# A transformer layer on one core: the causal mask moves from a PE product to a GpSimd clearing, with deeper rings and fewer VectorE operations in the first stage

## Chip, core and metric

One core of a Trainium2 chip runs the whole layer. The metric is the device time of one execution in microseconds; the kernel before takes 2691.55 us (median of three runs, 2686.87 to 2695.32). The engines are TensorE (PE, matmul), VectorE (DVE), ScalarE (ACT), GpSimd (POOL) and SyncE (SP, which here only issues DMAs). Each takes its instructions in order.

## What is computed

One layer over 2048 positions of width 1024, in float32, cut to what matters here:

```python
a = rms_norm(h, pre_mix_g)
q, k, v, f, u_sg, v_sg = split(a @ w_in)
c = cumsum(log_sigmoid(f + f_bias))                     # per head
logits = q @ k.T * 64 ** -0.5 + c[t] - c[s]             # 8 heads of 64, causal
y_att = softmax(where(k_pos <= q_pos, logits, -inf)) @ v
u, v = gelu(u_sg), layer_norm(gelu(v_sg), ln_g, ln_b)
y_sg = u * (tril(w_s) @ v + b_s)                        # chunks of 128 positions
h = h + rms_norm(concat(rms_norm(y_att), rms_norm(y_sg)) @ w_out)
h = h + rms_norm(square(relu(rms_norm(h) @ w1)) @ w2)
h = h + sigmoid(h @ w_g + b_g) * (p @ w_pe)
```

## The kernel before

Products are done in three parts (`mm3`, L104 to L106): each operand is split into a rounded high half and the rest, and high x high, high x low and low x high are summed. ACT makes the high half of a weight (L96), POOL the low half (L100); of a value that comes out of PSUM, ACT makes the high half (L116) and DVE the low half (L117).

**First stage** (up to about 565 us): the projection by `w_in`, in four blocks of 512 positions. Each block has six groups of columns (`GROUPS`, L326) of four accumulations; the first three (344 wide) give the gating value `gv`, a mixed one, and the forget logits with the rest of `u`; then come q, k and v (512 wide). In the text a "group" counts these accumulations, 0 to 23, two PSUM places (`pacc`) turn about. What else a block does hangs on that count: the layer norm from accumulation 8 (L409 to L418), the square sums and scaling of the next block's rows from 11 (`x_norm`, L279 to L296), the log-sigmoid at 11 (L374 to L393), the gating products from 14. The forget logits get their bias on DVE as they come out of PSUM (L357), and the gelu of the same accumulator follows on ACT (L358). The raw weights go through three places (`wrp`), results on their way to DRAM through two (`stg`).

Between these matmuls `maxima` (L142) is interleaved for the block before: it finds each query's largest logit. It loads key tiles (`KM`, two places, L165) and query tiles (`QM`) by DMAs on ACT's queue, multiplies (L169), and DVE takes maxima from PSUM (L172; on the diagonal tile the part left of the diagonal square by L172, and the square itself, plus the mask `dmask`, by L175).

**Second stage** (about 565 to 1115 us): attention, the output projection, and the maxima of the last block. `scores` (L637) does one tile of 128 keys by up to 512 queries: two products into PSUM (L644, L647), on a diagonal tile (`by_pe`, all four blocks since `MASKB` is 4) a third one that adds `dmask` (L649), the exponential on ACT (L651), its high half on ACT or DVE (L659, L657), the low half on DVE (L660). `weigh` (L663) multiplies by the values (L672 to L674). Scores run four steps ahead (`LA`); PSUM has two places for them. There are 320 steps, 128 of them on the diagonal.

**The rest**: the feed-forward part and the gate, which the change does not touch.

A scheduler orders the instructions of each engine, so code that stands later can be issued earlier.

Of the kernel before, what the change touches and what calls it, by code (L numbers as in the profile page):

```python
# [9 lines left out]
F32 = mybir.dt.float32  # L10
F32R = mybir.dt.float32r
# [9 lines left out]
H = 8  # L21
# [13 lines left out]
def trunk(ctx, tc, x, p, w_in, f_bias, sg_ln_g, sg_ln_b, sg_w, sg_b, att_out_g, sg_out_g,  # L35
# [4 lines left out]
    def pool(stack, name, bufs=1, space=None, side="left"):  # L40
# [36 lines left out]
                     base=0, channel_multiplier=1)  # L77
    ident_r = const1.tile([P, P], F32R, name="ident_r")
    ve.tensor_copy(ident_r, ident)

# [47 lines left out]
    def place_m():  # L128
# [4 lines left out]
        return p.tile([P, 512], F32, name="pM" if p is pM else "pM3")  # L133
    NKM = 2
    KM = [mst.tile([P, TB], F32R, name=f"KM{e}") for e in range(NKM)]
# [3 lines left out]
    for t in QM:  # L139
        ve.memset(t[HD:HD + 2].bitcast(F32), 1.0)  # L140

    def maxima(b):  # L142
# [12 lines left out]
        ve.tensor_copy(c0_all[:, b], ps[:, :H])  # L155
        n = 0
        for h in range(H):
            q = QM[h % 2]
            sc.dma_start(q[:HD].bitcast(F32), qS[b, h, :HD])
            mx = msm.tile([P, 4, 6], F32, name="mx")  # L160
            po.memset(mx, NEG)
            for c in range(b + 1):
                km = KM[n % NKM]
                n += 1
                sc.dma_start(km[:HD + 2].bitcast(F32), kS[c, h, HD:])  # L165
                for tt in range(4):
                    w = TB if c < b else P * (tt + 1)
                    ps = place_m()
                    pe.matmul(ps[:, :w], q[:, tt * P:(tt + 1) * P], km[:, :w], start=True, stop=True)  # L169
                    full = w if c < b else w - P  # L170
                    if full:
                        ve.tensor_reduce(mx[:, tt, c:c + 1], ps[:, :full], AX.X, ALU.max)  # L172
                    if c == b:
                        dg = ps[:, w - P:w]
                        ve.tensor_tensor_reduce(out=dg, in0=dg, in1=dmask, scale=1.0, scalar=NEG,  # L175
                                                op0=ALU.add, op1=ALU.max, accum_out=mx[:, tt, 5:6])
                    yield
            if last is not None:
                rows(*last)
            m = msm.tile([P, 4], F32, name="m")  # L180
            ve.tensor_reduce(m, mx, AX.X, ALU.max)
            ve.tensor_scalar(m, m, -1.0, c0_all[:, b, h:h + 1], ALU.mult, ALU.subtract)
            mh = msm.tile([P, 2, 4], F32R, name="mh")
            ve.tensor_copy(mh[:, 0], m)
# [36 lines left out]
    with ExitStack() as ph:  # L221
        cst = pool(ph, "cst1", 1)
        stg = pool(ph, "stg", 2)
        small = pool(ph, "small1", 2)
        wrp = pool(ph, "wrp", 3)
        wsp = pool(ph, "wsp", 12)
# [20 lines left out]
        def prep_consts():  # L247
            sy.dma_start(fb, f_bias[0].partition_broadcast(P))
            sy.dma_start(g_sgo, sg_out_g[0].rearrange("(k p) -> p k", p=P))
            sy.dma_start(lng, sg_ln_g[0].partition_broadcast(P))  # L250
            sy.dma_start(lnb, sg_ln_b[0].partition_broadcast(P))
            sy.dma_start(sgb, sg_b[0].rearrange("g t -> t g"))
            ve.memset(csum[:, 0], 0.0)
            ve.memset(ones, 1.0)
            po.affine_select(out=upper, in_=ones, pattern=[[1, P]], compare_op=ALU.is_ge, fill=0.0,
                             base=0, channel_multiplier=-1)
# [22 lines left out]
        def x_norm(st, parts, rest=None):  # L279
            ss = st["ss"]  # L280
            for t0, t1 in parts:
# [13 lines left out]
                for tt in range(t0, t1):  # L295
                    ve.tensor_scalar(st["xs"][tt], st["xs"][tt], r[:, tt - t0:tt - t0 + 1], None, ALU.mult)  # L296

# [30 lines left out]
        def block(b, aT, hooks, fill, first=None):  # L328
# [18 lines left out]
            def uv_done(tt, ps):  # L347
# [3 lines left out]
                ve.tensor_scalar(mu[:, tt:tt + 1], mu[:, tt:tt + 1], -1.0 / AW, None, ALU.mult)  # L351
                ve.tensor_scalar(gv[:, tt], gv[:, tt], mu[:, tt:tt + 1], None, ALU.add)
                junk = sg1.tile([P, 512], F32, name="junk")
                sc.activation(junk, gv[:, tt], AF.Square, accum_out=ss[:, tt:tt + 1])

            def fu_done(tt, ps):
                ve.tensor_tensor(zf[:, tt], ps[:, :H], fb, ALU.add)  # L357
                sc.activation(ug[:, tt, :336], ps[:, H:344], AF.Gelu_apprx_tanh)  # L358
# [15 lines left out]
            def log_sigmoid():  # L374

                ve.tensor_scalar(e, zf, -1.0, None, ALU.mult)
                ve.tensor_tensor(e, zf, e, ALU.min)
                sc.activation(e, e, AF.Sigmoid)
# [3 lines left out]
                ve.tensor_tensor(s2, s_, s_, ALU.mult)  # L382
                ve.tensor_scalar(pl, s2, 1.0 / 17, 1.0 / 15, ALU.mult, ALU.add)
                for k in (13, 11, 9, 7, 5, 3, 1):
                    ve.tensor_tensor(pl, pl, s2, ALU.mult)
                    ve.tensor_scalar(pl, pl, 1.0 / k, None, ALU.add)
# [22 lines left out]
            def layer_norm():  # L409

                r = rstd_of(small, ss, 4, AW, "lnr")
                for tt in range(4):
                    ve.scalar_tensor_tensor(gv[:, tt], gv[:, tt], r[:, tt:tt + 1], lng, ALU.mult, ALU.mult)
                    ve.tensor_tensor(gv[:, tt], gv[:, tt], lnb, ALU.add)
                    po.tensor_scalar(vn[:, 0, tt], gv[:, tt], 1.0, 0.0, ALU.mult, ALU.add)
# [221 lines left out]
    def scores(k, j):  # L637
# [7 lines left out]
        diag = j >= 4 * b  # L645
        by_pe = diag and b < MASKB
        pe.matmul(ps[:, off:], KA[:, js], QB[e][:, off:], start=False, stop=not by_pe)  # L647
        if by_pe:
            pe.matmul(ps[:, off:off + P], dmask_r, ident_r, start=False, stop=True)  # L649
        pr = pp.tile([P, TB], F32, name="pr")  # L650
        sc.activation(pr[:, off:], ps[:, off:], AF.Exp, bias=bias_of(b)[:, j, h:h + 1])  # L651
        if diag and not by_pe:
            po.affine_select(out=pr[:, off:off + P], in_=pr[:, off:off + P], pattern=[[1, P]],
# [983 lines left out]
```

## Time and profile before

| | |
|---|---|
| median of three runs | 2691.55 us |
| the profiled execution | 2682.36 us |
| its span, first to last instruction | 2680.6 us |
| PE busy | 2610.0 us (97%) |
| DVE, ACT, POOL busy | 1843.5, 1341.6, 806.6 us |
| granted PE clock, mean | 0.992 |

A row of a group reads: line, engine, operation, output and inputs, shapes and count, then busy time in us and the mean in ns of one, then the idle time of the engine just before these instructions and what ended it. A wait reads: who waited, for whom, us in total, times, the longest. The order of time gives start and duration in us, with the idle time ahead of an instruction in brackets. Matmuls overlap one another, so the sum of their durations is more than the time that they take; what one costs is read from the start of the next.

### The profile page before, as it was taken

To read this page: it belongs to the slowest core of one execution; us is meant where nothing else is said; L and a number is where in the kernel's file an instruction comes from. 1 tells how busy PE (TensorE), PEld (TensorE's weight loads), DVE (VectorE), ACT (ScalarE), POOL (GpSimd) and SP (SyncE) were. 2 spreads that over 40 slices of the span, in tenths; PEclk is the share of its full clock that TensorE was granted. 3 is DMA by queue.
4 is the path that set the end of the run, shared out by engine and by line. 5 is a ranking of instruction groups with operands and counts; after the bars stand their busy time and mean duration, and the time that the engine had idled before them with its cause. 6 is when DMAs were issued, how large, how long until landed. Compare 5 with 4: busy or idle time off the path is not lost.

```text
span 2680.6 us, 37427 instructions
## 1 busy us (share of the span) xinstructions
PE 2610.0 (97%) x12316; PEld 2123.4 (79%) x12316; DVE 1843.5 (69%) x3214; ACT 1341.6 (50%) x2632; POOL 806.6 (30%) x695
## 2 busy tenths in 40 slices
PE   8999999999999999989999999999999999999999
PEld 7797978777677777767787788888888888888887
DVE  5547586866877655588888677677786596875443
ACT  6443433358877777655555455445435544453111
POOL 5444343410000100244434223236360171401211
PEclk9999999999999999999999999999999999999999
DMA  5565756588977876455665854447466644673331
GB/s 168 149 186 142 204 143 170 139 219 213 230 190 189 182 180 148 128 173 202 207 200 178 305 178 148 148 148 272 152 196 218 197 155 131 215 246 112 110 120 61
DMA packets 440083, 472.62 MB, mean 176 GB/s; under 512 B 155088, under 2 KB 269520, under 8 KB 439888
## 3 DMA queue, kind: packets, MB, share of 16 engines
q1 hardware_dynamic: 429651, 454.16, 57.5%
q10 hardware_dynamic: 10237, 16.07, 2.2%
q8 instruction: 97, 1.59, 0.3%
q14 instruction: 98, 0.80, 0.1%
HBM read 336.28 MB, written 133.82 MB: 175 GB/s over the span
## 4 chain that ended last, share of the span: by engine, by line
PE 53%; DVE 2%; DMA 1%; issue 0%; POOL 0%; ACT 0%; SPq 0%; DVEq 0%; ACTq 0%
PE pf L106 17%; PE pf L105 17%; PE pf L104 17%; DMA w1raw<-in_w_ff_dram 1%; PE pf L1485 1%; DVE w1p L999 0%; DMA B<-jS 0%; DVE ws L1183 0%; PE pf L1023 0%; DVE C L999 0%; DVE hq L1202 0%; PE pf L1478 0%; DVE z L750 0%; DVE v L1242 0%; DVE B L999 0%
## 5 line engine op out<-in xcount | busy, mean ns | idle before, releaser
L104 PE MATMUL pf<-B,w1p 128*128 128x512 f32 x752 | 298.4, 397 | 5.0 <-ACT w1p L996 3.9
L106 PE MATMUL pf<-B,w1p 128*128 128x512 f32 x752 | 296.7, 395 | 5.2 <-DVE w1p L999 5.1
L105 PE MATMUL pf<-B,w1p 128*128 128x512 f32 x752 | 297.3, 395 | 0.0
L1210 POOL TENSOR_TENSOR hq<-hq,hq 128x512 f32<-128x512 f32 x128 | 197.4, 1552 | 327.8 <-ACT hq L1204 292.1
L660 DVE TENSOR_TENSOR hl<-pr,hl 128x512 fp32r<-128x512 f32 (+1 forms) x320 | 193.0, 612 | 101.7 <-ACT hl L659 88.4
L100 POOL TENSOR_TENSOR wsp<-wraw,wsp 128x344 fp32r<-128x344 f32 (+1 forms) x176 | 199.5, 1150 | 190.0 <-ACT wsp L96 177.1
L651 ACT ACTIVATE pr<-pS,bias 128x512 f32<-128x512 f32 (+1 forms) x320 | 196.3, 622 | 101.2 <-PE pS L647 65.5
L172 DVE TENSOR_REDUCE mx<-pM 128x1 f32<-128x512 f32 (+3 forms) x288 | 169.8, 597 | 72.9 <-PE pM L169 72.0
L104 PE MATMUL pacc<-wsp,wide 128*128 128x344 f32 (+1 forms) x480 | 166.7, 347 | 9.9 <-ACT ug L358 6.8
L104 PE MATMUL pf<-R,L 128*128 128x512 f32 x452 | 176.1, 390 | 0.0
L105 PE MATMUL pf<-R,L 128*128 128x512 f32 x452 | 176.1, 390 | 0.0
L106 PE MATMUL pf<-R,L 128*128 128x512 f32 x452 | 176.0, 389 | 0.0
L106 PEld LDWEIGHTS pf<-B,w1p 128*128 128x128 f32 x752 | 142.0, 189 | 40.2 <-DVE w1p L999 7.8
L104 PEld LDWEIGHTS pf<-B,w1p 128*128 128x128 f32 x752 | 141.6, 188 | 39.5 <-ACT w1p L996 4.6
L105 PEld LDWEIGHTS pf<-B,w1p 128*128 128x128 f32 x752 | 141.8, 189 | 31.4
L106 PE MATMUL pacc<-wsp,wide 128*128 128x344 f32 (+1 forms) x480 | 162.6, 339 | 0.6 <-DVE wide L117 0.6
L105 PE MATMUL pacc<-wsp,wide 128*128 128x344 f32 (+1 forms) x480 | 162.4, 338 | 0.0
L659 ACT CAST hl<-pr 128x512 fp32r<-128x512 f32 (+3 forms) x272 | 146.4, 549 | 6.7 <-PE pO L674 0.8
L999 DVE TENSOR_TENSOR L<-lr,L 128x512 fp32r<-128x512 f32 x113 | 98.8, 874 | 70.2 <-ACT L L996 69.8
L996 ACT CAST L<-lr 128x512 fp32r<-128x512 f32 x113 | 70.2, 621 | 152.2 <-PE pf L105 117.5
L999 DVE TENSOR_TENSOR w1p<-ws,w1p 128x512 fp32r<-128x512 f32 (+1 forms) x136 | 120.6, 890 | 30.0 <-ACT w1p L996 28.0
L996 ACT CAST w1p<-w1raw 128x512 fp32r<-128x512 f32 (+1 forms) x123 | 73.3, 598 | 127.2 <-PE pf L105 124.5
(446 smaller groups left out, 7191.7 us busy)
## 6 DMA issues: line engine op xcount, KB each, us to landing
hidC<-hq SPq DMA_DIRECT2D x224, 256.0 KB
lr<-hidC SPq DMA_DIRECT2D x224, 256.0 KB
w1raw<-in_w_ff_dram SPq DMA_DIRECT2D x64, 512.0 KB
w1raw<-in_w_ff_dram SPq DMA_DIRECT2D x128, 256.0 KB
wraw<-in_w_in_dram SPq DMA_DIRECT2D x96, 256.0 KB
wraw<-in_w_in_dram SPq DMA_DIRECT2D x88, 172.0 KB
KM<-kS ACTq DMA_DIRECT2D x80, 132.0 KB
jS<-C SPq DMA_DIRECT2D x19, 512.0 KB
```

Of the source, the lines that this page charges most:

```text
L100: e.tensor_tensor(dst[:, 1], src, dst[:, 0].bitcast(F32), ALU.subtract)
L104: pe.matmul(ps, l[0], r[0], start=first, stop=False)
L105: pe.matmul(ps, l[0], r[1], start=False, stop=False)
L106: pe.matmul(ps, l[1], r[0], start=False, stop=last)
L172: ve.tensor_reduce(mx[:, tt, c:c + 1], ps[:, :full], AX.X, ALU.max)
L651: sc.activation(pr[:, off:], ps[:, off:], AF.Exp, bias=bias_of(b)[:, j, h:h + 1])
L659: sc.copy(hl[:, 0, off:], pr[:, off:])
L660: ve.tensor_tensor(hl[:, 1, off:], pr[:, off:], hl[:, 0, off:].bitcast(F32), ALU.subtract)
L996: sc.copy(dst[:, 0], src)
L999: (po if lo == "pool" else ve).tensor_tensor(dst[:, 1], src, dst[:, 0].bitcast(F32), ALU.subtract)
L1210: po.tensor_tensor(t, x, y, op)
L1485: pe.transpose(ps[:, kk], hts[t][g][:, kk * P:(kk + 1) * P], ident)
```

## The change

In `scores` the mask product goes; instead POOL writes zeros above the diagonal of the exponentials, before they are split. In the maxima the diagonal tile is handled whole: one operation adds a mask as wide as the tile (`wmask`, zeros and `dmask` at its end) and takes the maximum. The key tiles get four places, and key and query loads are issued two tiles and one head ahead. In the first stage `wrp` has six places and `stg` three; the scaling of the rows goes to ACT (in block 0, half of it); the bias of the forget logits is added once for four tiles, and ACT copies the logits out of PSUM; the layer norm subtracts the mean and multiplies by the gain in one operation, without waiting for the deviation, and the square sum takes the mean as a bias; the log-sigmoid's polynomial has one operation per term; a tile of ones goes.

```diff
-    NKM = 2
+    NKM, LEAD = 4, 2
...
+    wmask = mst.tile([P, TB], F32, name="wmask")
+    ve.memset(wmask[:, :TB - P], 0.0)
+    ve.tensor_copy(wmask[:, TB - P:], dmask)
...
+        def load_k(i):
+            h, c = divmod(i, b + 1)
+            if h < H:
+                sc.dma_start(KM[i % NKM][:HD + 2].bitcast(F32), kS[c, h, HD:])
...
             for c in range(b + 1):
                 km = KM[n % NKM]
+                load_k(n + LEAD)
+                if c == b:
+                    load_q(h + 1)
                 n += 1
-                sc.dma_start(km[:HD + 2].bitcast(F32), kS[c, h, HD:])
...
-                    full = w if c < b else w - P
-                    if full:
-                        ve.tensor_reduce(mx[:, tt, c:c + 1], ps[:, :full], AX.X, ALU.max)
-                    if c == b:
-                        dg = ps[:, w - P:w]
-                        ve.tensor_tensor_reduce(out=dg, in0=dg, in1=dmask, scale=1.0, scalar=NEG,
-                                                op0=ALU.add, op1=ALU.max, accum_out=mx[:, tt, 5:6])
+                    if c < b:
+                        ve.tensor_reduce(mx[:, tt, c:c + 1], ps, AX.X, ALU.max)
+                    else:
+                        ve.tensor_tensor_reduce(out=ps[:, :w], in0=ps[:, :w], in1=wmask[:, TB - w:], scale=1.0, scalar=NEG,
+                                                op0=ALU.add, op1=ALU.max, accum_out=mx[:, tt, c:c + 1])
...
-        stg = pool(ph, "stg", 2)
+        stg = pool(ph, "stg", 3)
-        wrp = pool(ph, "wrp", 3)
+        wrp = pool(ph, "wrp", 6)
...
-                    ve.tensor_scalar(st["xs"][tt], st["xs"][tt], r[:, tt - t0:tt - t0 + 1], None, ALU.mult)
+                    for hf in range(2):
+                        xh, rt = st["xs"][tt][:, hf * 512:(hf + 1) * 512], r[:, tt - t0:tt - t0 + 1]
+                        if rest is not None and not hf:
+                            ve.tensor_scalar(xh, xh, rt, None, ALU.mult)
+                        else:
+                            sc.activation(xh, xh, AF.Copy, scale=rt)
...
-                ve.tensor_scalar(gv[:, tt], gv[:, tt], mu[:, tt:tt + 1], None, ALU.add)
-                sc.activation(junk, gv[:, tt], AF.Square, accum_out=ss[:, tt:tt + 1])
+                sc.activation(junk, gv[:, tt], AF.Square, bias=mu[:, tt:tt + 1], accum_out=ss[:, tt:tt + 1])
...
-                ve.tensor_tensor(zf[:, tt], ps[:, :H], fb, ALU.add)
+                sc.copy(zf[:, tt], ps[:, :H])
...
-                for k in (13, 11, 9, 7, 5, 3, 1):
-                    ve.tensor_tensor(pl, pl, s2, ALU.mult)
-                    ve.tensor_scalar(pl, pl, 1.0 / k, None, ALU.add)
+                for k in (15, 13, 11, 9, 7, 5, 3):
+                    ve.scalar_tensor_tensor(pl, pl, 1.0 / k, s2, ALU.add, ALU.mult)
...
-                    ve.scalar_tensor_tensor(gv[:, tt], gv[:, tt], r[:, tt:tt + 1], lng, ALU.mult, ALU.mult)
-                    ve.tensor_tensor(gv[:, tt], gv[:, tt], lnb, ALU.add)
+                    ve.scalar_tensor_tensor(gv[:, tt], gv[:, tt], mu[:, tt:tt + 1], lng, ALU.add, ALU.mult)
+                    ve.scalar_tensor_tensor(gv[:, tt], gv[:, tt], r[:, tt:tt + 1], lnb, ALU.mult, ALU.add)
...
-        by_pe = diag and b < MASKB
-        pe.matmul(ps[:, off:], KA[:, js], QB[e][:, off:], start=False, stop=not by_pe)
-        if by_pe:
-            pe.matmul(ps[:, off:off + P], dmask_r, ident_r, start=False, stop=True)
+        pe.matmul(ps[:, off:], KA[:, js], QB[e][:, off:], start=False, stop=True)
         pr = pp.tile([P, TB], F32, name="pr")
         sc.activation(pr[:, off:], ps[:, off:], AF.Exp, bias=bias_of(b)[:, j, h:h + 1])
-        if diag and not by_pe:
+        if diag:
             po.affine_select(out=pr[:, off:off + P], in_=pr[:, off:off + P], pattern=[[1, P]],
                              compare_op=ALU.is_ge, fill=0.0, base=0, channel_multiplier=-1)
```

How this moves the instructions, at two places. The rows give the line in the kernel that they belong to (before or after the change), the operation, the output and the inputs.

The first place is the end of block 0, where the forget logits come out of PSUM. ACT's order before, with `ug` the gelu of the logits' accumulator, `junk` the square sums of the next block's rows `xt`, `wsp` the weights:

```order
L358 ACTIVATE ug_177<-pacc_756 128x336
L290 ACTIVATE junk_1057,xss_674<-xt_681 128x512
L290 ACTIVATE junk_1059,xss_674<-xt_681 128x512
L96 CAST wsp_911<-wraw_909 128x512
L358 ACTIVATE ug_177<-pacc_787 128x336
L96 CAST wsp_916<-wraw_914 128x512
L96 CAST wsp_921<-wraw_919 128x512
L358 ACTIVATE ug_177<-pacc_818 128x336
```

ACT's order there after the change, where `zf` is the copy of the logits and `xr` the reciprocal root that comes from POOL:

```order
L303 ACTIVATE junk_1057,xss_678<-xt_685 128x512
L374 COPY zf_313<-pacc_760 128x8
L375 ACTIVATE ug_181<-pacc_760 128x336
L314 ACTIVATE xt_679<-xt_679,xr_882 128x512 x2
L314 ACTIVATE xt_681<-xt_681,xr_965 128x512 x2
L314 ACTIVATE xt_683<-xt_683,xr_1007 128x512 x2
L374 COPY zf_313<-pacc_791 128x8
L375 ACTIVATE ug_181<-pacc_791 128x336
L94 CAST wsp_909<-wraw_907 128x512
```

Each gelu now has its copy just ahead of it on the same engine, and between the second and the third pair stand six halves of scaling.

DVE's order at the same place before, with `lnr` the reciprocal deviation, `gv` and `vn` the layer norm:

```order
L110 TENSOR_SCALAR lnr_750<-lnss_305 128x4
L413 SCALAR_TENSOR_TENSOR gv_178<-gv_178,lnr_750,lng_164 128x512 x2
L357 TENSOR_TENSOR zf_307<-pacc_723,fb_163 128x8
L414 TENSOR_TENSOR gv_178<-gv_178,lnb_165 128x512 x2
L413 SCALAR_TENSOR_TENSOR gv_178<-gv_178,lnr_750,lng_164 128x512
L417 TENSOR_TENSOR vn_308<-gv_178,vn_308 128x512 x2
L414 TENSOR_TENSOR gv_178<-gv_178,lnb_165 128x512
L357 TENSOR_TENSOR zf_307<-pacc_756,fb_163 128x8
```

DVE's order there after the change:

```order
L368 TENSOR_TENSOR mu_312<-s1_310 128x1
L369 TENSOR_SCALAR mu_312<-mu_312 128x1
L108 TENSOR_SCALAR lnr_754<-lnss_311 128x4
L429 SCALAR_TENSOR_TENSOR gv_182<-gv_182,mu_312,lng_169 128x512
L430 SCALAR_TENSOR_TENSOR gv_182<-gv_182,lnr_754,lnb_170 128x512 x2
L433 TENSOR_TENSOR vn_314<-gv_182,vn_314 128x512
L430 SCALAR_TENSOR_TENSOR gv_182<-gv_182,lnr_754,lnb_170 128x512
```

The row with the gain (L429) no longer needs `lnr`; three of its four stand ahead of this piece. No row with `zf` and `pacc` is left on DVE.

The second place is the first diagonal tiles of the second stage. PE's order before, with `pS` the scores, `pM` the maxima:

```order
L644 MATMUL pS_6143<-QS0_6092,KS_6085 128x512
L647 MATMUL pS_6143<-QB0_6089,KA_6084 128x512
L649 MATMUL pS_6143<-ident_r_91,dmask_86 128x128
L644 MATMUL pS_6154<-QS0_6092,KS_6085 128x384
L647 MATMUL pS_6154<-QB0_6089,KA_6084 128x384
L649 MATMUL pS_6154<-ident_r_91,dmask_86 128x128
```

PE's order there after the change:

```order
L660 MATMUL pS_6052<-QS0_6001,KS_5994 128x512
L660 MATMUL pS_6063<-QS0_6001,KS_5994 128x384
L185 MATMUL pM_6119<-KM2_102,QM1_105 128x512
L662 MATMUL pS_6052<-QB0_5998,KA_5993 128x512
L662 MATMUL pS_6063<-QB0_5998,KA_5993 128x384
```

Two products per tile are left of three. POOL's order at the same place before, with the clearing of the maxima's places `mx` and small powers (`ar`):

```order
L552 MEMSET V_6086 128x32 x2
L563 MEMSET KA_6084 64x512 x7
L161 MEMSET mx_7309 128x24
L161 MEMSET mx_7949 128x24
L161 MEMSET mx_8316 128x24
L111 TENSOR_TENSOR ar_8018<-ar_8018,mhalf_75 128x1
```

POOL's order there after the change, with `pr` the exponentials:

```order
L579 MEMSET KA_5993 64x512 x7
L568 MEMSET V_5995 128x32 x2
L666 AFFINE_SELECT pr_6055<-pr_6055 128x128
L666 AFFINE_SELECT pr_6066<-pr_6066 128x128
L666 AFFINE_SELECT pr_6075<-pr_6075 128x128
L666 AFFINE_SELECT pr_6084<-pr_6084 128x128
L666 AFFINE_SELECT pr_6163<-pr_6163 128x128
```

One clearing per diagonal tile now stands in POOL's queue, ahead of the clearings of `mx`.

More of the change, by code (lines that the diff above doesn't have):

```diff
@@ L77, in trunk @@
                      base=0, channel_multiplier=1)
-    ident_r = const1.tile([P, P], F32R, name="ident_r")
-    ve.tensor_copy(ident_r, ident)
     def bcast(pool, name, v, n):
@@ L156, in maxima, with load_q @@
         n = 0
+        def load_k(i):
+            h, c = divmod(i, b + 1)
+            if h < H:
+                sc.dma_start(KM[i % NKM][:HD + 2].bitcast(F32), kS[c, h, HD:])
+        def load_q(h):
+            if h < H:
+                sc.dma_start(QM[h % 2][:HD].bitcast(F32), qS[b, h, :HD])
+        load_q(0)
+        for i in range(LEAD):
+            load_k(i)
         for h in range(H):
             q = QM[h % 2]
-            sc.dma_start(q[:HD].bitcast(F32), qS[b, h, :HD])
-            mx = msm.tile([P, 4, 6], F32, name="mx")
+            mx = msm.tile([P, 4, NB], F32, name="mx")
             po.memset(mx, NEG)
@@ L241, in trunk @@
         sgb = cst.tile([P, H], F32, name="sgb")
-        ones = cst.tile([P, P], F32, name="ones")
         upper = cst.tile([P, P], F32, name="upper")
@@ L253, in prep_consts @@
             ve.memset(csum[:, 0], 0.0)
-            ve.memset(ones, 1.0)
-            po.affine_select(out=upper, in_=ones, pattern=[[1, P]], compare_op=ALU.is_ge, fill=0.0,
+            ve.memset(upper, 1.0)
+            po.affine_select(out=upper, in_=upper, pattern=[[1, P]], compare_op=ALU.is_ge, fill=0.0,
                              base=0, channel_multiplier=-1)
@@ L374, in log_sigmoid @@
             def log_sigmoid():
-                ve.tensor_scalar(e, zf, -1.0, None, ALU.mult)
-                ve.tensor_tensor(e, zf, e, ALU.min)
+                ve.tensor_tensor(zf, zf, fb.unsqueeze(1).broadcast_to([P, 4, H]), ALU.add)
+                ve.scalar_tensor_tensor(e, zf, -1.0, zf, ALU.mult, ALU.min)
                 sc.activation(e, e, AF.Sigmoid)
@@ L382, in log_sigmoid @@
                 ve.tensor_tensor(s2, s_, s_, ALU.mult)
-                ve.tensor_scalar(pl, s2, 1.0 / 17, 1.0 / 15, ALU.mult, ALU.add)
-                for k in (13, 11, 9, 7, 5, 3, 1):
-                    ve.tensor_tensor(pl, pl, s2, ALU.mult)
-                    ve.tensor_scalar(pl, pl, 1.0 / k, None, ALU.add)
-                ve.scalar_tensor_tensor(pl, pl, -2.0, s_, ALU.mult, ALU.mult)
+                ve.tensor_scalar(pl, s2, 1.0 / 17, None, ALU.mult)
+                for k in (15, 13, 11, 9, 7, 5, 3):
+                    ve.scalar_tensor_tensor(pl, pl, 1.0 / k, s2, ALU.add, ALU.mult)
+                ve.scalar_tensor_tensor(pl, pl, 1.0, s_, ALU.add, ALU.mult)
                 ve.tensor_scalar(zf, zf, 0.0, None, ALU.min)
-                ve.tensor_tensor(pl, pl, zf, ALU.add)
+                ve.scalar_tensor_tensor(pl, pl, -2.0, zf, ALU.mult, ALU.add)
                 ve.tensor_copy(car[:, 0], csum[:, b])
@@ L397, in run_sum @@
                 pe.matmul(ps[:, :32], upper, pl.rearrange("p a h -> p (a h)"), start=True, stop=False)
-                pe.matmul(ps[:, :32], ones, car[:, 0:4].rearrange("p a h -> p (a h)"), start=False, stop=True)
+                pe.matmul(ps[:, :32], upper[:, P - 1:P].broadcast_to([P, P]), car[:, 0:4].rearrange("p a h -> p (a h)"), start=False, stop=True)
                 ve.tensor_copy(c_all[:, 4 * b:4 * b + 4].rearrange("p a h -> p (a h)"), ps[:, :32])
@@ L815, in trunk @@
     YSQL, YNOL = 2, 7
-    MASKB = 4
     PREPT = 54
```

## The prediction

> **What bounds the kernel now.** I read the page's busy shares first, then the windows by 20 us, then who TensorE (PE) waited for in the first stage, and there the instructions in order of time.
>
> ```profile
> PE 2610.0 (97%) x12316; PEld 2123.4 (79%) x12316; DVE 1843.5 (69%) x3214; ACT 1341.6 (50%) x2632; POOL 806.6 (30%) x695
> ...
> 40.00:60.00 20.00, 19.45 (x125) 19.17 (x123) 8.05 (x17) 11.65 (x35) 10.90 (x11) 1.00 0.46 127
> 60.00:80.00 20.00, 14.81 (x70) 12.89 (x71) 18.05 (x32) 10.50 (x24) 13.64 (x15) 0.91 0.27 77
> ...
> 200.00:220.00 20.00, 15.23 (x61) 12.15 (x60) 18.44 (x48) 7.61 (x17) 12.47 (x14) 0.83 0.30 81
> ...
> 340.00:360.00 20.00, 17.90 (x88) 14.06 (x86) 20.00 (x44) 9.24 (x21) 12.01 (x13) 1.00 0.39 108
> ...
> 500.00:520.00 20.00, 16.69 (x73) 12.29 (x72) 18.29 (x58) 7.38 (x13) 7.72 (x7) 1.00 0.58 160
> ```
>
> PE is busy 97% of the span, so the kernel is as long as PE's work and its gaps. The window columns are PE, PEld, VectorE (DVE), ScalarE (ACT), GpSimd (POOL), PE's granted clock, DMA share and GB/s. In the quiet window PE starts 125 matmuls in 20 us. Once in each of the four blocks of the first stage it drops to 61 to 88, and there DVE is busy 18.0 to 20.0 us of 20 while ACT does 7.4 to 10.5: DVE bounds these stretches. In two of them the granted clock falls too. What PE waited for up to 575 us (total, times, longest):
>
> ```profile
> PE pacc L104 <- ACT ug L358: 9.0, 5, 2.5
> PE pM L169 <- DVE mx L172: 4.8, 8, 1.3
> PE pacc L104 <- DVE stg L117: 4.3, 3, 1.9
> ```
>
> The first names ACT, but the order of time shows who held ACT (start, duration):
>
> ```profile
> 197.92 1.75 POOL L100 TENSOR_TENSOR wsp<-wraw,wsp 128x512 fp32r<-128x512 f32 x1
> ...
> 198.44 1.79 DVE L414 TENSOR_TENSOR gv<-gv,lnb 128x512 f32<-128x512 f32 x1
> ...
> 202.20 0.15 DVE L357 TENSOR_TENSOR zf<-pacc,fb 128x8 f32<-128x8 f32 x1
> ...
> 202.39 0.45 ACT L358 ACTIVATE ug<-pacc 128x336 f32<-128x336 f32 x1 [2.95 <-DVE zf L357]
> 202.61 0.68 DVE L414 TENSOR_TENSOR gv<-gv,lnb 128x512 f32<-128x512 f32 x1
> 202.74 0.62 ACT L290 ACTIVATE junk<-xt 128x512 f32<-128x512 f32 x1
> 202.89 0.46 PE L104 MATMUL pacc<-wsp,wide 128*128 128x344 f32 x1 [2.52 <-ACT ug L358]
> ```
>
> A 0.15 us add on DVE (the forget logits, L357) stands behind the layer norm; the gelu behind it on ACT sat 2.95 us, and PE 2.52 us for its accumulator. So all three rows are DVE's queue.
>
> **The change part by part. First stage.** What leaves DVE's hot stretch, by the groups:
>
> ```profile
> L413 DVE SCALAR_TENSOR_TENSOR gv<-gv,lnr,lng 128x512 f32<-128x512 f32 x16 | 21.0, 1315 | 4.5 <-POOL lnr L111 4.5
> L296 DVE TENSOR_SCALAR xt<-xt,xr 128x1024 f32<-128x1024 f32 x16 | 18.0, 1127 | 3.3 <-POOL xr L111 3.0
> L417 DVE TENSOR_TENSOR vn<-gv,vn 128x512 fp32r<-128x512 f32 x16 | 16.4, 1027 | 1.6 <-POOL vn L415 1.6
> L414 DVE TENSOR_TENSOR gv<-gv,lnb 128x512 f32<-128x512 f32 x16 | 13.2, 829 | 0.0
> L352 DVE TENSOR_SCALAR gv<-gv,mu 128x512 f32<-128x512 f32 x16 | 10.2, 636 | 0.5
> L386 DVE TENSOR_SCALAR lpl<-lpl 128x32 f32<-128x32 f32 x28 | 7.9, 281 | 0.5
> L111 POOL TENSOR_TENSOR xr<-xr,mhalf 128x1 f32<-128x1 f32 x16 | 10.8, 680 | 15.0 <-DVE xr L110 7.9 <-DVE xss L293 6.3 <-PE pM L169 0.8
> ```
>
> After the statistics of the layer norm DVE had 1.315 + 0.829 + 1.027 = 3.17 us per tile. The change does the multiplication by the gain before the deviation is known (L413's length, in place of L352's 0.636 us), so 1.315 + 1.027 = 2.34 us stay, 3.3 us less per block. The scaling of the next block's rows, 4 x 1.127 = 4.5 us, goes to ACT, seven small operations of the log-sigmoid are fused into others (7 x 0.281 = 2.0 us), and the four logit adds of 0.15 us become ACT copies. Together 10.4 us leave a stretch in which DVE is short of 18 to 20 us per 20. The diagonal maxima lose a separate reduction each; that helps the same queue, and I count it at nothing beyond this. With so much gone I take the three waits as gone: 9.0 + 4.8 + 4.3 = **-18.1 us**. The clock goes with them: (1 - 0.91) x 20 + (1 - 0.83) x 20 = **-5.2 us**. [...]
>
> The change puts a new wait in ACT's queue: six halves of scaling (0.62 us each, by L290's row) stand ahead of the third copy and gelu and wait for the powers on POOL, which stand behind the four layer norm roundings. From the statistics on: 4 x 2.34 + 3 x 0.68 + 2 x 0.62 + 0.45 = 13.1 us to that gelu. PE has four groups of 24 matmuls at 20 / 125 = 0.16 us, 15.4 us from the seventh group's end, less some 2 us until the statistics are there: 13.4. That is just even, so I charge 2 us in each of three blocks, **+6 us**, between nothing and 3 x 1.75 x 2 = 10.5 (two weight splits on POOL, of the length shown, ahead of a power).
>
> The deeper rings: six raw weight places instead of three and three staging places instead of two only let DMAs start earlier; no row of PE's list above names them, so nothing is booked, either way. At the start DVE clears two more key tiles and a wide mask before it may square x:
>
> ```profile
> 1.13 1.03 DVE L138 MEMSET KM<- 128x512 f32 x2
> ...
> 4.68 0.69 DVE L286 CUSTOM_DVE_ANT_0 gv<-xt 128x512 f32<-128x512 f32 x1 [0.25 <-DMA xt<-in_x_dram]
> ```
>
> 1.03 + some 0.4 (three quarters of one) - 0.25 of idle is at most +1.2, the halved scaling gives back a part: **+1 us**, down to 0. First stage: -18.1 - 5.2 + 6 + 1 = **-16.3**, from -23.3 to -11.6 by these ends.
>
> **Second stage.** The mask products:
>
> ```profile
> L649 PE MATMUL pS<-ident_r,dmask 128*128 128x128 f32 x128 | 30.6, 239 | 0.0
> ...
> 665.48 0.39 PE L647 MATMUL pS<-QB,KA 128*128 128x512 f32 x1
> 665.71 0.22 PE L649 MATMUL pS<-ident_r,dmask 128*128 128x128 f32 x1
> 665.77 0.39 PE L673 MATMUL pO<-hl,V 128*65 128x512 f32 x1
> ...
> 600.00:660.00 60.00, 7.55 (x32) 6.05 (x32) 1.00 0.83 214
> 660.00:720.00 60.00, 5.84 (x24) 4.73 (x24) 0.97 0.90 228
> ...
> 600.00:660.00 60.00, 59.69 (x342) 46.41 (x341) 39.25 (x88) 48.43 (x101) 0.12 (x1) 1.00 0.83 214
> 660.00:720.00 60.00, 54.76 (x300) 40.67 (x299) 51.11 (x112) 53.44 (x110) 0.12 (x1) 0.97 0.90 228
> ...
> PE pS L644 <- ACT pr L651: 6.1, 6, 2.0
> PE pM L169 <- DMA KM<-kS: 1.7, 1, 1.7
> ```
>
> Matmuls overlap, so the 239 ns are not the cost: the next one starts 0.06 us after, and 128 of them take 7.7 us of PE. The second pair of windows has all work, the first pair the mask products alone. In 660 to 720 us ACT does 53.4 of 60 us and PE already waits for its exponentials; there 24 products hide and their removal is worth nothing. The other 104 are worth 104 x 0.06 = **-6.2 us**. The fill of a key tile two ahead takes away the 1.7 us wait for one: **-1.7**.
>
> In place of the product POOL clears 128 triangles in the path exponential, rounding on ACT, subtraction on DVE:
>
> ```profile
> L255 POOL TENSOR_SCALAR_AFFINE_SELECT upper<-ones 128x128 f32<-128x128 f32 x1 | 0.6, 570 | 0.0
> L76 POOL TENSOR_SCALAR_AFFINE_SELECT dmask<-dmask 128x128 fp32r<-128x128 f32 x1 | 0.3, 293 | 0.0
> ...
> L660 DVE TENSOR_TENSOR hl<-pr,hl 128x512 fp32r<-128x512 f32 x224 | 152.9, 689 | 86.3 <-ACT hl L659 73.6 <-PE pM L106 7.5 <-PE pW L106 2.5
> ```
>
> POOL is idle there (0.12 us of 60), so I take 0.293 us, the row with nothing beside it. In ACT's order mostly two exponentials stand ahead of two roundings, so the first triangle is cleared under the second exponential. Where ACT has slack, nothing is lost, since scores run four steps ahead; in the full stretch I charge half of 24 x 0.293 = 7.0: **+3.5**, between 0 and 7.0. Second stage: **-4.4**, from -9.4 (all 128, no stall) to -0.9.
>
> Sum: -16.3 - 4.4 = -20.7 us on the profiled execution's 2682.36, that is 2661.7; on the median of the timed runs, 9.2 us above it, **2671**.
>
> **The rivals.** (1) *The wait moves to ACT's queue*: the scaling behind POOL's powers costs all that DVE's queue did, and the first stage stays as it is; 2691.55 - 4.4 = 2687. The even balance of 13.1 against 13.4 us speaks for it, ACT's idle half of the hot stretches against. (2) *The triangles lengthen ACT's full stretch*, slower than before: from 600 to 720 us ACT has 120 - 48.43 - 53.44 = 18.1 us to spare and 56 triangles to wait for. With 0.570 us for a triangle behind a DVE subtraction of 0.689, each holds ACT 1.26 us: 70.5 - 18.1 = 52.4 us longer. Against that stand 16.3 from the first stage, 7.7 of masks and 1.7: 2691.55 + 52.4 - 25.7 = 2718. It starts at 18.1 / 56 = 0.32 us per triangle and makes the whole slower from (18.1 + 25.7) / 56 = 0.78. [...] Against the rival: two exponentials ahead. (3) *More than the forecast*: no new wait on ACT, and the exponential wait of 6.1 us goes as well; -18.1 - 5.2 - 7.7 - 1.7 - 6.1 = -38.8, 2653. (4) *The products cost their busy time*, 30.6 instead of 6.2 us: 2671 - 24.4 = 2647; the start times above speak against it.
>
> **How the numbers follow.** Forecast 0.65; (1) 0.13, (2) 0.06, (3) 0.13, (4) 0.03. The range reaches from (3), 2653, to 2688, just past (1), and leaves out (2), (4) and the edges. 0.3%, about what a measurement of this kernel can tell from no change, is 8.1 us. Faster: nearly all of the forecast, (3), (4) and a little of (1): 0.80; same: most of (1) and the weak end of the forecast: 0.13; slower: (2) and a little: 0.07.
>
> **What would show it.** Right: in the changed kernel's first stage the wait of PE for the gelu and for the maxima nearly gone, DVE clearly below 18 us in the four hot windows, no clock dip near 200 us, and PE's 660 to 720 us no better than before. Wrong: PE waiting there for a gelu that waits for POOL's powers (1), or ACT's roundings waiting 0.3 us and more for POOL with the stretch from 600 to 720 us longer (2); and wrong altogether if the first stage is shorter by under 8 us while its waits are gone.

## The result and the profile after the change

The changed kernel takes **2670.03 us** (median of four runs, 2668.16 to 2670.59), the kernel before in the same session 2689.24 (four runs, 2686.87 to 2695.32). The ratio is 0.9923, its 95% interval 0.9905 to 0.9942: faster by 0.8%. Forecast was 2671. The profiled execution of the changed kernel took 2670.59 us, its span is 2668.8 us.

The totals on the page of the changed kernel, and the stretches of 20 us that answer to those of before, with the first one added (columns as there):

```profile
PE 2602.6 (98%) x12188; PEld 2107.5 (79%) x12188; DVE 1803.9 (68%) x3047; ACT 1357.6 (51%) x2678; POOL 847.7 (32%) x823
```
```profile
0.00:20.00 20.00, 14.52 (x61) 11.58 (x61) 13.99 (x44) 15.41 (x40) 8.07 (x18) 0.91 0.89 266
...
60.00:80.00 20.00, 15.30 (x61) 12.62 (x60) 9.85 (x22) 12.68 (x25) 12.55 (x13) 0.83 0.25 67
...
200.00:220.00 20.00, 18.64 (x74) 14.76 (x75) 14.25 (x42) 10.93 (x22) 11.03 (x12) 0.91 0.54 152
...
340.00:360.00 20.00, 18.26 (x82) 14.48 (x81) 17.45 (x45) 9.20 (x18) 9.49 (x10) 1.00 0.60 170
...
480.00:500.00 20.00, 17.55 (x82) 13.81 (x80) 18.26 (x47) 10.41 (x20) 14.41 (x13) 1.00 0.60 162
```

VectorE (third busy column) is relieved in three of the four hot stretches: 18.05 to 9.85, 18.44 to 14.25, 20.00 to 17.45 us of 20. PE gains nothing from it in the first: 61 matmuls in 60 to 80 us instead of 70, at a granted clock of 0.83 instead of 0.91. What PE (and, below, ScalarE) waited for up to 575 and 560 us:

```profile
PE pacc L102 <- ACT ug L375: 6.7, 2, 4.7
PE pM L185 <- DVE mx L187: 4.4, 6, 1.2
PE pacc L102 <- DVE stg L115: 4.1, 3, 1.7
```
```profile
ACT xt L314 <- POOL xr L109: 20.0, 5, 6.6
```

The three names of the prediction are all still there, at 15.2 us where they had 18.1. The gelu now waits in ScalarE's own queue. In order of time at the worst place:

```profile
63.16 0.22 DVE L306 TENSOR_TENSOR xss<-xss 128x1 f32<-128x1 f32 x2
63.33 1.07 POOL L109 TENSOR_TENSOR xr<-xr,mhalf 128x1 f32<-128x1 f32 x2 [0.87 <-DVE xss L306]
...
63.91 3.78 ACT L314 ACTIVATE xt<-xt,xr 128x512 f32<-128x512 f32 x6 [6.65 <-POOL xr L109]
...
67.60 0.14 ACT L374 COPY zf<-pacc 128x8 f32<-128x8 f32 x1
67.64 0.44 ACT L375 ACTIVATE ug<-pacc 128x336 f32<-128x336 f32 x1
67.99 2.17 ACT L94 CAST wsp<-wraw 128x512 fp32r<-128x512 f32 x4
68.14 0.79 PE L102 MATMUL pacc<-wide,wsp 128*128 128x512 f32 x1 [4.70 <-ACT ug L375]
```

ScalarE stands 6.65 us at the first scaling of the next block's rows (L314) until GpSimd has the power, which itself waited for VectorE's square sums; then six halves run, and only then come the logits' copy and the gelu that free PE's accumulator. This is the mechanism of rival 1, in two of the three blocks where it can happen.

The two stages by the last matmul of the projection and the last weighing by values:

```profile
563.82 0.39 PE L106 MATMUL pacc<-wide,wsp 128*128 128x512 f32 x1
1115.76 0.22 PE L674 MATMUL pO<-hl,V 128*65 128x128 f32 x1
```
```profile
547.33 0.40 PE L104 MATMUL pacc<-wide,wsp 128*128 128x512 f32 x1
1101.95 0.28 PE L687 MATMUL pO<-hl,V 128*65 128x128 f32 x1
```

The first stage (above before, below after) ends 16.5 us earlier; the second, from the one matmul to the other, takes 551.9 us before and 554.6 after. On this pair alone the second stage lost 2.7 us. That is an accident of the one profile of before, as a second one shows (next section). The 16.5 us depend on it too: in the second profile, and in the kernel before with the triangles only, whose first stage is the same, the projection ends at 567.6 and 567.3 us, 20 us later than in the changed kernel.

### The profile page after: what moved, and what is told of

Same layout as the page of the kernel before. It is cut to its first block, busy times and chain, and to the rows that moved or that the text cites. A ratio compares the mean times of both kernels' runs of the same rounds, so it can differ in the third digit from the quotient of the medians.

```text
span 2668.8 us, 37153 instructions
## 1 busy us (share of the span) xinstructions
PE 2602.6 (98%) x12188; PEld 2107.5 (79%) x12188; DVE 1803.9 (68%) x3047; ACT 1357.6 (51%) x2678; POOL 847.7 (32%) x823
## 4 chain that ended last, share of the span: by engine, by line
PE 52%; DVE 2%; DMA 2%; issue 1%; POOL 1%; ACT 0%; SPq 0%; DVEq 0%; POOLq 0%; ACTq 0%
PE pf L104 17%; PE pf L103 17%; PE pf L102 17%; DMA w1raw<-in_w_ff_dram 2%; PE pf L1497 1%; DVE w1p L1011 1%; DVE ws L1195 0%; POOL hq L1222 0%; DVE B L1011 0%; PE pf L1035 0%; DMA x<-hS 0%; POOL tmp L1087 0%; DVE hq L1214 0%; DMA cS<-ws 0%; DVE z L763 0%
## 5 line engine op out<-in xcount | busy, mean ns | idle before, releaser
L98 POOL TENSOR_TENSOR wsp<-wraw,wsp 128x344 fp32r<-128x344 f32 (+1 forms) x176 | 193.0, 1130 | 116.4 <-ACT wsp L94 106.7
L187 DVE TENSOR_REDUCE mx<-pM 128x1 f32<-128x512 f32 x192 | 129.7, 685 | 41.5 <-PE pM L185 40.8
```

What stands on the lines that cost most here:

```text
L98: e.tensor_tensor(dst[:, 1], src, dst[:, 0].bitcast(F32), ALU.subtract)
L187: ve.tensor_reduce(mx[:, tt, c:c + 1], ps, AX.X, ALU.max)
```

## The experiments

The kernels were timed against the kernel before in the same session (its medians there 2690.89, 2692.83 and 2691.68 us). Differences below are of medians; between kernels of different sessions the ratios, times 2690, give up to some 2 us more or less (5.9 in place of 7.9 us for the rings, 16.4 in place of 14.8 for the late scaling, 3.2 in place of 5.1 for the mask products). For the rings and the mask products in the changed kernel the single times don't overlap with its own, but the intervals of the ratios do: the sign is likely, the size is rough. The last two columns are the places shown above, in each kernel's profiled execution: the end of the projection, and the length of the second stage from there.

| kernel | median us | ratio to before, 95% interval | projection ends | second stage |
|---|---|---|---|---|
| before, first and second profile | | | 563.8, 567.6 | 551.9, 562.1 |
| changed | 2670.03 | 0.9923 (0.9905 to 0.9942) | 547.3 | 554.6 |
| changed, mask product on PE | 2675.11 | 0.9935 (0.9913 to 0.9957) | 551.5 | 559.6 |
| changed, product in blocks 0, 1 | 2668.70 | 0.9913 (0.9892 to 0.9933) | 549.5 | 552.4 |
| before, triangles only | 2697.08 | 1.0018 (1.0008 to 1.0029) | 567.3 | 569.7 |
| before, keys ahead only | 2690.41 | 0.9998 (0.9985 to 1.0010) | 566.5 | 555.1 |
| before, keys and triangles | 2681.46 | 0.9962 (0.9948 to 0.9975) | 567.2 | 549.5 |
| changed, shallow rings | 2677.90 | 0.9945 (0.9926 to 0.9965) | 555.8 | 555.0 |
| before, deep rings only | 2691.54 | 1.0005 (0.9993 to 1.0017) | 567.8 | 565.0 |
| changed, scaling on VectorE | 2673.13 | 0.9929 (0.9913 to 0.9945) | 553.8 | 553.0 |
| changed, scaling after the gelu | 2655.21 | 0.9862 (0.9846 to 0.9877) | 532.2 | 554.5 |
| the same with shallow rings | 2662.36 | 0.9889 (0.9874 to 0.9903) | 542.9 | 551.8 |
| changed, four query places | 2673.36 | 0.9927 (0.9906 to 0.9947) | 548.9 | 555.9 |

### The second stage: is before's profile typical?

The kernel before, unchanged, for a second profile.

> The kernel before once more, for a second profile. Theory A, the profile that the prediction read was a lucky execution of the second stage: here PE waits 5 to 15 us for key tiles (1.7 there), and the span is 2685 to 2698 us (2680.6 there). Theory B, it was typical: under 3 us, and a span of 2679 to 2684 us.

Span 2692.4 us (2694.15 us in all), the second stage 562.1 us instead of 551.9. PE's wait for key tiles after 565 us is 4.8 us, just under theory A's 5; the span is A's:

```profile
PE pM L169 <- DMA KM<-kS: 4.8, 3, 2.0
```

Three profiles have before's second stage in its code (both of these and the one with deep rings only): 551.9, 562.1, 565.0. Five have the changed one with all its edits there (changed, shallow rings, and the three with the scaling moved): 554.6, 555.0, 553.0, 554.5, 551.8. The means are 559.7 and 553.8, so by them the change takes about 6 us out of the second stage. That is an estimate: the three of before lie 13 us apart, the longest of them from an execution of 2701.11 us, the slowest of its kernel's twelve. The profile that the prediction read was the shortest of the three of before.

### The second stage: mask products, triangles, key tiles

The product put back into the changed kernel, in all query blocks, and in blocks 0 and 1 alone (`MASKB = 2`):

```diff
-        pe.matmul(ps[:, off:], KA[:, js], QB[e][:, off:], start=False, stop=True)
+        by_pe = diag and b < MASKB
+        pe.matmul(ps[:, off:], KA[:, js], QB[e][:, off:], start=False, stop=not by_pe)
+        if by_pe:
+            pe.matmul(ps[:, off:off + P], dmask_r, ident_r, start=False, stop=True)
...
-        if diag:
+        if diag and not by_pe:
```

> The changed kernel with the mask product back on PE in all four blocks (no triangle on GpSimd); all else as changed. Theory A (the 9.4 us that the changed kernel loses again between 547 and 700 us come from query tiles that arrive late, because their DMAs stand behind others in SP's queue; the triangles cost little): the first stage keeps its 16 us, the 128 products cost 128 x 0.06 = 7.7 us where PE is the bound, so about 6 us slower than the changed kernel, 2676. Theory B (ScalarE waits for the triangles, and that is the 9.4 us): these come back, the products cost some 6, so 2667. If a product cost its busy time (239 ns), it would be 2670 + 24 = 2694 or more.

> The changed kernel with the mask product on PE for query blocks 0 and 1 only (64 diagonal tiles, all before about 730 us); triangles on GpSimd for blocks 2 and 3. Theory A: the loss up to 700 us stays and 64 x 0.06 = 3.8 us come on top where PE is the bound, 2670 to 2674. Theory B: no triangle is left in that stretch, so 9 us come back less some 3 for products: 2664.

2675.11 us, theory A's figure, and 2668.70, between the two theories. All products are worth 3 to 5 us, so they don't cost PE their busy time (rival 4), nor do triangles hold ScalarE for a microsecond each (rival 2). In blocks 0 and 1 product and triangle come out alike.

Then the two edits alone, in the kernel before: the triangles (`MASKB = 0` there, which is all of the edit), the key tiles filled ahead (`NKM, LEAD = 4, 2` with `load_k` and `load_q`), and both.

> The kernel before with the mask product taken out of all four query blocks and GpSimd clearing the triangles, nothing else of the change. Putting the product back into the changed kernel cost 5 us. Theory A, the products cost PE 0.04 to 0.06 us each and the triangles are nearly hidden: 2690.9 - 5 = 2686 us (2683 to 2688). Theory B, the triangles hold ACT in the first two blocks, and only the kernel's other edits cover that: 2690 to 2693 us. The rival of the prediction in which each triangle costs over a microsecond of ACT would give more than 2705 us.

> The kernel before with four key tiles, filled two ahead, and the queries a head ahead, nothing else of the change. In the prediction's profile PE waits 1.7 us for a key tile, in two other kernels with the old loading 8.1 and 14.5 us. Theory A, that wait varies from execution to execution and the profile of before was a lucky one: the loading alone gives 5 to 10 us, 2683 to 2688 us, and the wait is nowhere in the trace. Theory B, the prediction's size is right: 1 to 2 us, 2690 to 2692 us, not to be told from before (2692.8).

> The kernel before with the key tiles filled ahead as in the run beside it and, besides, the triangles cleared by GpSimd in place of the mask product. With the old loading the triangles alone made the kernel 4 us slower. Theory A, they did so because the old key loads stand in ScalarE's queue behind the roundings that wait for GpSimd, at the moment when the tile is needed: with the loads two tiles ahead the triangles gain the 5 us that they gain in the changed kernel, 4 to 6 us below the run beside it. Theory B, the roundings' stall itself costs the time: 3 to 5 us above the run beside it.

The triangles alone make it *slower* (+0.18%, 4 to 5 us), which was past both theories; the keys ahead alone do nothing that can be measured (theory B, the prediction's size); both together take 10 us off, 9 us below the keys alone. PE's waits for key tiles after 565 us with the triangles and the old loading, and the longest of them in order of time:

```profile
PE pM L169 <- DMA KM<-kS: 14.5, 5, 4.2
```
```profile
860.32 0.30 ACT L659 CAST hl<-pr 128x128 fp32r<-128x128 f32 x1 [0.39 <-POOL pr L653]
...
861.32 0.29 ACTq L165 DMA_DIRECT2D KM<-kS  x1
...
871.92 0.44 PE L169 MATMUL pM<-KM,QM 128*128 128x128 f32 x1 [4.24 <-DMA KM<-kS]
```

With both edits this wait is nowhere in the list. So the loads ahead are what lets the triangles pay. The way in which I had put it does not hold, though: I expected the load to be issued late, behind roundings that wait for GpSimd, but at the longest wait the one rounding ahead of it waited 0.39 us, and PE got the tile 10.6 us after the issue. There the time lies between the issue and the landing; the other four waits were not followed. Why the old loading costs 14.5 us with triangles and 1.7, 4.8 and 8.1 us without (three profiles) was not tried further.

### The first stage: the rings

`wrp` 6 to 3 and `stg` 3 to 2 in the changed kernel; the reverse in the kernel before.

> The changed kernel with the raw weight ring back at 3 places (from 6) and the staging ring back at 2 (from 3); key tiles keep their 4 places. The prediction booked nothing for these rings: 2670, within 2 us. Rival: the rings carry a part of the first stage's 16.5 us (3.6 us of it are gained in the first 36 us, where the prediction had a loss of 1): 4 to 8 us slower, 2674 to 2678, lost before 40 us and at the ends of the blocks.

> The kernel before with six raw weight places and three staging places, nothing else of the change. Putting the shallow rings back into the changed kernel cost 7.9 us of its first stage. Theory A, the deeper rings are worth this much by themselves: 2690.9 - 8 = 2683 us (2680 to 2686), with the first stage's last matmul about 8 us earlier. Theory B, they only pay once VectorE is relieved, because VectorE's queue holds the stretches in which the rings would help: 2688 to 2692 us. The prediction booked them at nothing, which is B's number.

2677.90 us, 7.9 us slower than the changed kernel, and 2691.54 us, no different from before. The prediction booked nothing for the rings, since no row of PE's list named them. ScalarE's list up to 560 us did, had I looked for raw weights there (61.3 us in the profile that I read). In the second profile of before, in before with deep rings, and in the changed kernel with shallow and with deep ones

```profile
ACT wsp L96 <- DMA wraw<-in_w_in_dram: 67.2, 48, 4.5
```
```profile
ACT wsp L96 <- DMA wraw<-in_w_in_dram: 7.5, 9, 2.7
```
```profile
ACT wsp L94 <- DMA wraw<-in_w_in_dram: 65.5, 52, 4.2
```
```profile
ACT wsp L94 <- DMA wraw<-in_w_in_dram: 5.1, 9, 1.3
```

The rings take 60 us of these waits away in either kernel (8 to 11 us of them come back as waits of the `wide` halves for raw weights). In the one before that time is slack, where VectorE is relieved it is worth 8 us: this is a gain that the rings have only together with the other edits. That they do nothing in the first because VectorE's queue ends last there fits the prediction's windows, but was not tested by itself, and the two rings were not tried apart.

### The first stage: where the row scaling stands

In the changed kernel the scaling is issued only behind the last gelu of the block; and, in another kernel, it goes back to VectorE in one operation per tile.

```diff
-                for tt in range(t0, t1):
+                with (tc.issue_after(fu_last["i"].ins) if late else ExitStack()):
+                  for tt in range(t0, t1):
...
-                sc.activation(ug[:, tt, :336], ps[:, H:344], AF.Gelu_apprx_tanh)
+                fu_last["i"] = sc.activation(ug[:, tt, :336], ps[:, H:344], AF.Gelu_apprx_tanh)
```

> The changed kernel, but in every block the scaling of the next block's rows is issued only behind the last gelu of the gating value, so that no gelu stands behind a scaling that waits for GpSimd's powers. Theory A, the waits of PE for that gelu (6.7 us in all, 4.7 us of them at 68 us) are what the moved scaling costs: they go, and the whole is 3 to 6 us shorter, 2663 to 2667 us. Theory B, the wait only changes its name (the rows are then scaled too late for the transposes, or PE next waits for a wide half or a maximum): 2668 to 2674 us.

> The changed kernel with the scaling of the rows back on VectorE, all else as changed. Theory A, as in the prediction: the 4 x 1.13 us per block that left VectorE are 4.5 of the 10.4 us by which its hot stretch got shorter, so that 4 to 10 us of the first stage come back, 2673 to 2679 us, with PE's waits for a gelu behind VectorE and for the maxima growing. Theory B, the other edits and the rings already relieve it enough, and the scaling on ACT costs as much in waits for GpSimd's powers as it saves on VectorE: 2666 to 2671 us, with the wait of 4.7 us at 68 us gone.

With the scaling behind the gelu it takes 2655.21 us, 14.8 less than the changed kernel and 1.4% less than before: theory A in kind, at over twice its size. It is the fastest kernel here. Its waits of PE up to 575 us, the first rows and the one for staging, and three of its stretches:

```profile
PE pM L185 <- DVE mx L187: 4.9, 7, 1.2
PE pM L185 <- DVE car L411: 1.9, 1, 1.9
PE pacc L102 <- ACT wide L114: 1.9, 3, 1.4
...
PE pacc L102 <- DVE stg L115: 0.3, 1, 0.3
```
```profile
60.00:80.00 20.00, 19.64 (x91) 15.94 (x90) 13.70 (x37) 12.85 (x24) 14.19 (x14) 1.00 0.48 129
200.00:220.00 20.00, 19.66 (x95) 15.64 (x95) 12.18 (x37) 10.20 (x19) 12.32 (x12) 1.00 0.78 207
340.00:360.00 20.00, 20.00 (x101) 16.47 (x100) 10.94 (x28) 7.03 (x12) 10.89 (x11) 1.00 0.78 218
```

The waits for the gelu are gone (6.7 us), those for staging nearly so (3.8), and the clock is full in all of these stretches; from 60 to 80 and 200 to 220 us it had cost (0.17 + 0.09) x 20 = 5.2. Together 15.7 us, against 15.2 by which the projection ends earlier; the two need not match, since smaller waits differ as well. With the scaling on VectorE it takes 2673.13 us, 3 us more than the changed kernel, the lower edge of theory A; the single times (2669.20 to 2676.96) overlap with those of the changed kernel, so this is not told from no difference. So moving the scaling to ScalarE was worth at most some 3 us as it was placed, and 18 us where no gelu stands behind it.

The late scaling with the old rings:

> The changed kernel with the scaling behind the last gelu (2655.2 us) and the old rings, three raw weight places and two staging places. In the kernel before the deeper rings were worth nothing, in the changed kernel 8 us. Theory A, they pay wherever VectorE no longer sets the pace: at least as much here, 2663 to 2668 us. Theory B, they only bridge the stalls of ScalarE behind the scaling, which are gone here: 2655 to 2659 us.

2662.36 us, 7.2 more: just below theory A's range, and above B's. So the rings don't only bridge ScalarE's stalls behind the scaling; they pay in both kernels in which VectorE is relieved.

### The beginning of the second stage

Against the first profile of before, the changed kernel's lead is 16 us at its first weighing (553.11 against 569.40 us) and 7 us at 700. PE waited there for query tiles (2.1 and 0.9 us for `QS` and `QB` between 565 and 700 us), whose loads are issued by SyncE behind others that wait (4.39 us at 674.14):

```profile
674.14 4.39 SPq L593 DMA_DIRECT2D xt<-in_w_out_dram  x1
...
681.39 0.32 SPq L647 DMA_DIRECT2D QB<-qS  x1
...
687.02 1.22 PE L662 MATMUL pS<-QB,KA 128*128 128x512 f32 x2 [0.88 <-DMA QB<-qS]
```

So a fourth place for them (`NQ = 4`) was tried.

> The changed kernel with four places for query tiles in the second stage instead of three (NQ = 4), so that each head's query DMAs are issued one head earlier. Theory A: PE's waits for QS and QB (2.5 and 0.9 us, and ScalarE's 8.3 and 4.1 us of idle time behind them) go, with the clock dips at 580 and 680 us: 5 to 8 us faster, 2662 to 2665. Theory B: no query tile was late for the bound, 2670.

2673.36 us: no gain. The lead at 700 us is larger, and goes in the next 20 us, in which the DMA share is full:

```profile
680.00:700.00 20.00, 19.21 (x93) 12.33 (x91) 16.50 (x33) 18.07 (x37) 1.44 (x4) 1.00 0.77 205
700.00:720.00 20.00, 13.52 (x49) 7.57 (x48) 13.61 (x32) 9.34 (x20) 1.53 (x5) 0.91 1.01 225
```

That the transfers are late either way is how I read it; it was not tested further. And with the second profile of before there is little left to explain.

## Why the prediction came out right, and which of its steps did not

The sum for the first stage was -16.3 us, measured -16.5 against the profile that the prediction read and -20 against the second one; for the second stage -4.4, measured about -6 by the means above. The total is right; the first stage's terms are not. The signs named for being right failed with them: PE still waits for the gelu, VectorE is busy 18.26 us in the fourth stretch, and the clock dips near 200 us. The sign named for rival 1, a gelu behind POOL's powers, is there.

- **"I take the three waits as gone", -18.1 us: failed.** They are at 15.2 us. Less work on VectorE took its queue away as the reason, and ScalarE's queue took its place for the gelu; the maxima stay at 4.4 to 4.9 us even in the fastest kernel. What did get shorter is spread out: the rings' 8 us, the first 20 us ((0.91 - 0.74) x 20 = 3.4 us of clock), and small stalls that I did not separate. Nor were the edits that relieve VectorE (layer norm, log-sigmoid, bias, maxima) tried one by one.
- **The new wait in ScalarE's queue, +6 us: right in the row, mis-sized in the time.** The row says 6.7 us. Taking it away brought 14.8 us, because the staging waits went with it (3.8 us) and a wait of two microseconds can cost nearly twice: PE stood 2.04 us, then had a clock of 0.52 for 3.4 us, by an estimate 3.7 us together (last section). The even balance of 13.1 to 13.4 us missed that the power itself comes behind VectorE's square sums.
- **The clock, -5.2 us: failed for the change, right as a price.** In the two stretches it is still 5.2 us after. With the waits gone it came back fully. Tying it to the waits was right; that the waits would go was not. The clock fell to 0.51 and 0.52 after single waits of 2.04, 2.17 and 2.52 us, though not after every one of that length (last section).
- **Deeper rings, 0: failed.** -8 us in the changed kernel. The step "no row of PE's list names them, so nothing is booked" looked at the engine that ends last before the edit, not after.
- **Start of the kernel, +1: failed in sign.** In the first 20 us the changed kernel starts 61 matmuls at a clock of 0.91 (above); before had 46 at 0.74. With the scaling on VectorE it is in between (the two rows below); with the shallow rings it is 62 at 0.91, so the rings are not the reason.

```profile
0.00:20.00 20.00, 14.02 (x46) 10.53 (x47) 14.98 (x41) 12.41 (x33) 9.29 (x19) 0.74 0.87 250
```
```profile
0.00:20.00 20.00, 14.59 (x53) 11.39 (x54) 16.20 (x44) 12.72 (x35) 9.29 (x19) 0.83 0.86 255
```

- **Mask products, -6.2, and triangles, +3.5: right in sign, and together about right in size.** The exchange, -2.7 by my terms, is -3 to -5 in the changed kernel; the runs don't separate its two parts. Most of the triangles' 48.6 us is hidden. ScalarE's waits for them between 555 and 700 us, then the group of the triangles, then their shortest, median and longest duration in ns:

```profile
ACT hl L672 <- POOL pr L666: 6.7, 17, 0.6
```
```profile
L666 POOL TENSOR_SCALAR_AFFINE_SELECT pr<-pr 128x128 f32<-128x128 f32 x128 | 48.6, 383 | 237.3 <-ACT pr L664 224.1 <-DVE hr_all L771 11.8 <-DVE hl L673 0.9
```
```profile
L666 POOL TENSOR_SCALAR_AFFINE_SELECT pr<-pr x128: 289/296/834, 551.4 to 1100.5; 128x128 f32<-128x128 f32 x128
```

  A triangle takes 0.383 us in the mean, mostly the 0.29 of my row and at worst more than the 0.57 of the other, and above the 0.32 from which rival 2 was to start. It did not: 6.7 us of waiting by ScalarE in that stretch is what was left uncovered. That each triangle stands behind a whole subtraction of VectorE, 0.689 us, was rival 2's assumption and no run shows it: the median is 0.296 us, and the longest, 0.834, is under the 1.26 that it reckoned with. Nor had the row of 0.293 us nothing beside it: it began at 1.38 us, and VectorE's L138 ran from 1.13 to 2.16.
- **Key tiles, -1.7: right in size alone, wrong in role.** Filled ahead they give nothing by themselves, and 13 to 14 us together with the triangles (from 4 to 5 us lost to 9 gained).
- **The bridge to the median, +9.2 us:** the first profile of before was a short execution, by 10 us in its second stage and by 4 in its first. Adding the same difference to the forecast put it right in the mean.

Rival 1's mechanism was there, at 14.8 us; the rings, the start and the rest made up for it. The forecast is near because these errors cancel, not because its terms held. Rivals 2 and 4 fell. Rival 3's time, 2653, is nearly what the late scaling reaches (2655), for both of its reasons in part: the gelu no longer waits behind the scaling, and PE's wait for exponentials after 565 us, 6.1 us before, is 1.8. The forecast had left it at 6.1; in the changed kernel it is 1.4 already:

```profile
PE pS L660 <- ACT pr L664: 1.4, 4, 0.6
```

## What to carry to other kernels

When work moves from a full engine to an idle one, look at what stands *behind* it in the new queue: the same scaling was worth at most some 3 us ahead of the gelus and 18 us behind them. A buffer's depth is to be judged against the engine that will end last after the change; here it was worth nothing before and 8 us after, and GpSimd's triangles cost 4 to 5 us or gave 9 depending on an edit that did nothing measurable alone. One profile of before can be 10 us off in one stage: take a second before explaining a few microseconds there.

## What the runs showed of the hardware

After several waits of two microseconds and more PE was granted half its clock for 3.41 us: in before the clock is 1.00 up to 73.43 us, 0.50 from 73.45 and 1.00 again from 76.86. By an estimate such a stretch costs 3.41 / 2 = 1.7 us more. Stretches of before (behind waits of 2.17 and 2.52 us that ended at 73.29 and 202.89) and of the changed kernel (behind the wait of 4.70 us that ended at 68.14, and one of 2.04 at 200.39):

```profile
73.40:76.90 3.50, 3.50 (x9) 2.74 (x10) 2.79 (x7) 1.01 (x3) 3.28 (x4) 0.51 0.20 68
203.30:206.70 3.40, 3.40 (x14) 3.24 (x13) 3.39 (x11) 1.67 (x6) 1.04 (x2) 0.52 0.28 78
```
```profile
67.30:74.20 6.90, 6.06 (x14) 4.78 (x15) 2.95 (x5) 4.40 (x12) 5.53 (x6) 0.51 0.35 86
200.30:203.70 3.40, 3.31 (x8) 2.69 (x9) 0.44 (x4) 3.40 (x8) 2.62 (x3) 0.52 0.09 11
```

The granted clock is 0.51 to 0.52 in all four. The third is twice as long as the others: at the longest wait the clock is 0.50 from 67.29 us, while PE still stands, to 74.12. One stretch of 3.41 us takes 1.7 / 20 = 0.085 off the mean clock of a slice of 20 us, so the 0.91, 0.83 and 0.74 of the slices above are as much as one, two and three of them. In before a wait of 1.56 us was not followed by one, one of 2.17 us was (the two rows below); the late scaling, in whose list no wait up to 575 us is longer than 1.9 us, has a clock of 1.00 in the three hot stretches shown above.

```profile
67.07 0.43 PE L104 MATMUL pacc<-wsp,wide 128*128 128x344 f32 x1 [1.56 <-ACT ug L358]
73.29 0.69 PE L104 MATMUL pacc<-wide,wsp 128*128 128x512 f32 x1 [2.17 <-ACT ug L358]
```

The length of a wait alone doesn't decide it here. In before the wait of 2.01 us that ended at 61.46 has a clock of 1.00 behind it, and so has one of 2.65 us in the kernel with the product in blocks 0 and 1. On the other side, before is granted 0.50 from 568.4 to 571.8 us, behind a wait of 1.28 us that ended at 568.19. The first two waits, each with the stretch behind it:

```profile
61.46 0.43 PE L104 MATMUL pacc<-wsp,wide 128*128 128x344 f32 x1 [2.01 <-ACT ug L358]
61.46:64.90 3.44, 3.44 (x22) 3.44 (x23) 3.44 (x5) 3.25 (x9) 3.29 (x3) 1.00 0.21 68
```
```profile
201.94 0.50 PE L104 MATMUL pacc<-wide,wsp 128*128 128x512 f32 x1 [2.65 <-ACT ug L377]
202.00:205.40 3.40, 3.40 (x15) 2.81 (x16) 0.29 (x3) 3.40 (x9) 2.78 (x3) 1.00 0.15 17
```

In before stretches of half clock begin at 73.44, 203.14, 216.79 and 568.37 us, in the changed kernel at 67.29 and 200.41. From the first to the others it is 38, 42 and 145 times 3.413 us in before (129.70, 143.35, 494.93), and 39 times in the changed kernel (133.12). What sets one wait apart from another of its length the runs don't show.

By an estimate from the rows above, a wait that was followed by half clock cost more than its own length: the one of 2.04 us 2.04 + 3.31 / 2 = 3.7, the one of 4.70 us 4.70 + 6.06 / 2 = 7.7.
